# Twelve lines at the two ends of an encoder trunk kernel: how x, the gains and the first weights are loaded, and who makes four of the first eight high parts and two of the last four sums

## The chip, the cores and the metric

The kernel runs on one core of one Trainium2 chip. The metric is the device time of one execution in microseconds (us): 1946.46 us before, the median of three runs (1946.46, 1948.36 and 1946.42). TensorE (PE) does the matmuls; VectorE (DVE), ScalarE (ACT) and GpSimd (POOL) work elementwise; the queues of SyncE (SP) and of ACT issue DMAs, which 16 DMA engines carry.

## The reference

Four layers over 256 positions of width 1024 in float32. Each layer is a SwiGLU block, a token mixer (attention, spatial gating, differential attention, attention again) and another SwiGLU block, each between two norms and added to x:

```python
for i in range(DEPTH):
    g = norm_g[i]
    x = x + 0.5 * rms_norm(swiglu(rms_norm(x, g[0]), ff1_w_in[i], ff1_w_out[i]), g[1])
    ...
    x = x + rms_norm(m, g[3])
    x = x + 0.5 * rms_norm(swiglu(rms_norm(x, g[4]), ff2_w_in[i], ff2_w_out[i]), g[5])
return x
```

The change touches only how the first `x * g[0]` is prepared and how the very last `x + ...` is added and sent out.

## The kernel before

x lives in SBUF as `xr`, 128 partitions by KD = 8 blocks (k = 0 to 7) of S = 256 positions. Every operand of a matmul is cut into a high part and a low part (float32r); a product is three matmuls: high by high, high weight by low x, low weight by high x. For weights, `Stream.split` does it piece by piece (a piece is 128 x 1024): ACT casts the high part (`w_hi`, line 126), DVE subtracts to get the low part (`w_lo`, line 129). Only piece 0 is cut in two halves of 512 columns, so that its first four blocks (k = 0 to 3) can be used before the rest. For x, `Normed.high` (ACT, line 319) multiplies a block by its gain and rounds, and `Normed.low` (DVE, line 334) makes the remainder; both write into `xp`.

The start. SP's queue issues, in this order: x blocks 0 and 1, the first half of piece 0, its second half, x blocks 2 to 4, x blocks 5 to 7, piece 1, then two pieces of the second weight tile; later weight tiles (line 103) wait for their buffer. ACT's queue issues all gains as one DMA (line 197). DVE halves two of the six gain vectors of each layer (line 227) as soon as the gains are there, before anything else that needs data. PE runs 19 matmuls on a constant tile, the fillers (line 237), then the first product (`project_pair`, line 526), block by block in the order of k for piece 0, with two, one or no fillers between its first matmuls (`DUMMY`); pieces 1 to 3 follow with no filler. `Normed.begin` sets the order on ACT and DVE: the high and low part of block 0, then `W.split()` for piece 0 (both halves), then blocks 1 to 7, then pieces 1 to 3 between the squares for the norm.

The end. After the last projection `finish` spreads the norm factor with a matmul (line 258). Then `Update.multiply` (line 473, DVE, reading the factor from PSUM) makes the update of two blocks, `Update.add` (line 479) adds it to `xr`, and SP sends those two blocks out (line 1188); a loop of four turns does this, with the multiply of the next two blocks issued ahead of the add of the present two. The updates lie in tiles with the tag `upd`, of which there are two buffers. The order on PE, DVE and ACT is the order in which the code is written; on SP and POOL a scheduler sets it.

In what follows m(a) is the multiply and a(a) the add of blocks a and a + 1, with a = 0, 2, 4, 6.

Of the kernel before, what the change touches and what calls it, by code (L numbers as in the profile page):

```python
# [13 lines left out]
ALU = mybir.AluOpType  # L14
# [5 lines left out]
DEPTH = 4  # L20
KD = D // P
# [9 lines left out]
PIECE = 1024  # L31
# [25 lines left out]
def encoder_trunk_kernel(  # L57
# [14 lines left out]
    nc = tc.nc  # L72
# [121 lines left out]

    xr = act.tile([P, KD, S], F32, tag="xr", name="xr")
    g_sb = const.tile([P, DEPTH, 6, KD], F32, name="g_sb")
    nc.scalar.dma_start(g_sb, gains)
    W.load()

    def load_x(a, b):  # L200
        nc.sync.dma_start(xr[:, a:b, :], x_t[:, a:b, :])

    def load_w(c, a, b):
        nc.sync.dma_start(W.raws[c][:, a:b], w[c][:, a:b])

    load_x(0, 2)
    load_w(0, 0, PIECE // 2)
    load_w(0, PIECE // 2, PIECE)
    load_x(2, 5)
    load_x(5, KD)  # L210
    load_w(0, PIECE, WC)
    W.load()
    load_w(1, 0, PIECE)
# [52 lines left out]
    class Normed:  # L266
# [36 lines left out]
        def begin(self, gain):  # L303

            for k in range(KD):
                self.high(gain, k, k + 1)
                self.low(gain, k, k + 1)
                if k == 0:
                    W.split()
            for i in range(3):  # L310
                W.split()
                W.settle()
                for a in ((0, 2, 4), (6,), ())[i]:
                    self.square(a)
            self.total()
# [149 lines left out]
    class Update:  # L465
# [9 lines left out]
            )  # L475
            self.t[a] = t

        def add(self, a, b):
            nc.vector.tensor_tensor(xr[:, a:b, :], xr[:, a:b, :], self.t.pop(a), op=ALU.add)  # L479

    LARGE = {"h0": 4 * D, "h1": 2 * D, "l0": 2 * D, "l1": 4 * D}

# [695 lines left out]
    update = None  # L1178
    for l in range(DEPTH):
        update = ffn(l, 0, update, Ahead(g_sb[:, l, 2, :], True))  # L1180
        update = mixers[l % 3](l, l // 3, update)
        update = ffn(l, 1, update, Ahead(g_sb[:, l + 1, 0, :]) if l + 1 < DEPTH else None)
    update.multiply(0, 2)
    for a in range(0, KD, 2):
        if a + 2 < KD:
            update.multiply(a + 2, a + 4)
        update.add(a, a + 2)
        nc.sync.dma_start(out[:, a:a + 2, :], xr[:, a:a + 2, :])


# [73 lines left out]
```

## Time and profile before

| | us |
|---|---|
| median of three runs | 1946.46 |
| the profiled execution, its own time | 1947.0 |
| span of that execution, first to last instruction | 1945.3 |
| TensorE busy in the span | 1931.1 (99%) |
| VectorE busy | 1378.4 (71%) |
| ScalarE busy | 1169.6 (60%) |
| GpSimd busy | 5.2 (under 1%) |

The span is the time between the first and the last instruction; 1.7 us of the execution lie around it. A busy share is an average over the whole span; the change concerns the first 13 us and the last 9 us, which have to be read by themselves.

### The profile page before, as it was taken

To read this page: it belongs to the slowest core of one execution; us is meant where nothing else is said; L and a number is where in the kernel's file an instruction comes from. 1 tells how busy PE (TensorE), PEld (TensorE's weight loads), DVE (VectorE), ACT (ScalarE), POOL (GpSimd) and SP (SyncE) were. 2 spreads that over 40 slices of the span, in tenths; PEclk is the share of its full clock that TensorE was granted. 3 is DMA by queue.
4 is the path that set the end of the run, shared out by engine and by line. 5 is a ranking of instruction groups with operands and counts; after the bars stand their busy time and mean duration, and the time that the engine had idled before them with its cause. 6 is when DMAs were issued, how large, how long until landed. Compare 5 with 4: busy or idle time off the path is not lost.

```text
span 1945.3 us, 30035 instructions
## 1 busy us (share of the span) xinstructions
PE 1931.1 (99%) x12402; PEld 1745.4 (90%) x12402; DVE 1378.4 (71%) x1883; ACT 1169.6 (60%) x1805; POOL 5.2 (0%) x19
## 2 busy tenths in 40 slices
PE   9999999999999999999999999999999999999998
PEld 8888999888988889888988899988898888999887
DVE  6775867866777577877677668786767766868763
ACT  6655657656655565756565565675656555656552
POOL 0000000000000000000000000000000000000000
PEclk9999999999999999999999999999999999999999
DMA  7555524655455543655455544255545554535551
GB/s 262 205 184 202 190 108 154 232 189 184 171 196 186 205 163 141 216 195 182 165 195 195 195 155 174 109 200 196 188 155 213 180 206 161 197 123 183 203 201 44
DMA packets 50393, 350.30 MB, mean 180 GB/s; under 512 B 5712, under 2 KB 5968, under 8 KB 9040
## 3 DMA queue, kind: packets, MB, share of 16 engines
q1 hardware_dynamic: 48096, 341.86, 49.0%
q10 hardware_dynamic: 2160, 6.52, 0.9%
q8 instruction: 97, 1.59, 0.3%
q14 instruction: 40, 0.33, 0.1%
HBM read 347.31 MB, written 1.05 MB: 179 GB/s over the span
## 4 chain that ended last, share of the span: by engine, by line
PE 98%; DVE 1%; ACT 0%; DMA 0%; ACTq 0%; issue 0%; SPq 0%; DVEq 0%
PE pp_t L182 68%; PE pp_t L526 8%; PE pp_t L168 7%; PE pp_t L507 4%; PE pp_t L691 3%; PE pp_t L650 2%; PE pp_t L731 1%; PE pst_t L763 1%; PE pst_t L243 1%; PE pp_t L448 1%; PE pst_t L258 1%; PE pst_t L448 1%; PE pp_t L885 0%; PE pp_t L446 0%; DVE upd L473 0%; DMA w_raw<-in_w 0%
## 5 line engine op out<-in xcount | busy, mean ns | idle before, releaser
L129 DVE TENSOR_TENSOR w_lo<-w_raw,w_hi 128x1024 fp32r<-128x1024 f32 (+1 forms) x649 | 776.4, 1218 | 69.6 <-ACT w_hi L126 69.6
L126 ACT CAST w_hi<-w_raw 128x1024 fp32r<-128x1024 f32 (+1 forms) x649 | 668.9, 1046 | 160.1 <-PE pp_t L182 130.7
L182 PE MATMUL pp_t<-xp,w_hi 128*128 128x512 f32 x2560 | 613.7, 391 | 0.0
L182 PEld LDWEIGHTS pp_t<-xp,w_hi 128*128 128x128 f32 x2560 | 469.7, 188 | 90.4
L182 PEld LDWEIGHTS pp_t<-xp,w_lo 128*128 128x128 f32 x2560 | 329.0, 191 | 12.5
L182 PE MATMUL pp_t<-xp,w_lo 128*128 128x256 f32 x2560 | 334.6, 283 | 0.0
L597 DVE TENSOR_TENSOR gu<-pp_t,share 128x512 f32<-128x512 f32 x160 | 110.7, 692 | 206.1 <-ACT share L596 206.1
L596 ACT COPY share<-pp_t 128x512 f32<-128x512 f32 x160 | 93.6, 585 | 150.5 <-PE pp_t L182 149.5
L182 PE MATMUL pp_t<-h,w_hi 128*128 128x512 f32 x672 | 169.0, 391 | 0.0
L182 PE MATMUL pp_t<-l,w_hi 128*128 128x512 f32 x560 | 142.6, 391 | 0.0
L182 PEld LDWEIGHTS pp_t<-h,w_hi 128*128 128x128 f32 x672 | 122.1, 189 | 22.6
L567 ACT ACTIVATE gs<-gs 128x512 f32<-128x512 f32 x88 | 55.7, 633 | 141.5 <-DVE gs L566 141.5
L526 PE MATMUL pp_t<-xp,w_hi 128*128 128x256 f32 x832 | 123.8, 288 | 1.6 <-ACT xp L319 0.8
L182 PEld LDWEIGHTS pp_t<-l,w_hi 128*128 128x128 f32 x560 | 102.5, 188 | 21.1 <-DVE l L576 1.6
L526 PEld LDWEIGHTS pp_t<-xp,w_hi 128*128 128x128 f32 x832 | 111.1, 193 | 3.7 <-ACT xp L319 1.0
L364 DVE TENSOR_TENSOR yg<-pp_t,share 128x256 f32<-128x256 f32 x56 | 23.8, 425 | 108.8 <-ACT share L363 108.8
L182 PEld LDWEIGHTS pp_t<-h,w_lo 128*128 128x128 f32 x672 | 91.1, 191 | 5.0
L182 PE MATMUL pp_t<-h,w_lo 128*128 128x256 f32 x672 | 95.1, 282 | 0.0
L182 PE MATMUL pp_t<-l,w_lo 128*128 128x256 f32 x560 | 80.6, 283 | 0.0
L319 ACT ACTIVATE xp<-xr,g_sb 128x256 fp32r<-128x256 f32 x96 | 44.8, 504 | 56.4 <-DVE xr L479 54.0
L182 PEld LDWEIGHTS pp_t<-l,w_lo 128*128 128x128 f32 x560 | 75.3, 191 | 2.9
L526 PE MATMUL pp_t<-xp,w_lo 128*128 128x256 f32 x416 | 73.8, 284 | 0.0
(196 smaller groups left out, 2255.7 us busy)
## 6 DMA issues: line engine op xcount, KB each, us to landing
w_raw<-in_w SPq DMA_DIRECT2D x322, 1024.0 KB, 4.8
l<-in_a_bias ACTq DMA_DIRECT2D x8, 512.0 KB, 8.3
w_raw<-in_w SPq DMA_DIRECT2D x3, 512.0 KB, 8.5
out_y<-xr SPq DMA_DIRECT2D x4, 256.0 KB, 2.1
xr<-in_x_t SPq DMA_DIRECT2D x2, 384.0 KB, 6.7
w_raw<-in_w SPq DMA_DIRECT2D x2, 256.0 KB, 4.6
l<-in_b_ws ACTq DMA_DIRECT2D x1, 512.0 KB, 5.4
l<-in_b_ln_g ACTq DMA_DIRECT2D x1, 512.0 KB, 7.2
```

Of the source, the lines that this page charges most:

```text
L126: nc.scalar.copy(hi[:, cols], raw[:, cols])
L129: nc.vector.tensor_tensor(lo[:, cols], raw[:, cols], hi[:, cols].bitcast(F32), op=ALU.subtract)
L168: nc.tensor.matmul(o, w_[:, at + i, :], x(k)[:, low, :], start=(start and i == 0 and m == 0), stop=(stop and k == ks[-1] and m == 2),)
L182: nc.tensor.matmul(o[:, 0:S] if low else o, (wl if low else wh)[:, at + i, :], x(k)[:, 0, :] if low else x(k), start=(start and i == 0 and ...
L319: nc.scalar.activation(self.h[:, k, :], xr[:, k, :], AF.Copy, scale=gain[:, k:k + 1])
L448: nc.tensor.matmul(o[:, 0:S], w_, x, start=first, stop=last, skip_group_check=True)
L507: nc.tensor.matmul(o, part[:, k, :], n.x[:, k, int(low), :], start=((k, low) == JOIN[0] and i == 2 and part is ws[i][0]), stop=((k, low) = ...
L526: nc.tensor.matmul(o, part[:, k, :], n.x[:, k, low, :], start=(at == 0), stop=(at == 3 * KD - 1))
L567: nc.scalar.activation(gs, gs, AF.Silu)
L596: nc.scalar.copy(share, ps[:, :, S:2 * S])
L597: nc.vector.tensor_tensor(at.t[:, e], ps[:, :, 0:S], share, op=ALU.add)
L691: nc.tensor.matmul(self.ps[:, t, :], xs[:, kk, t * P:(t + 1) * P], ws, start=((kk, low) == self.order[0] and ws is wh and not (t == 0 and ...
```

## The change

Loads: x comes as two halves (blocks 0 to 3, blocks 4 to 7) with the whole of piece 0 as one DMA between them. The gains come as three DMAs on ACT's queue: the vector that the first norm needs, the other five of layer 0, and layers 1 to 3. High parts: the odd blocks 1, 3, 5 and 7 of the first norm are multiplied on GpSimd. Piece 0 is cast after block 2 and not after block 0. End: the adds of blocks 0 and 1 and of blocks 4 and 5 go to GpSimd.

```diff
-    nc.scalar.dma_start(g_sb, gains)
+    nc.scalar.dma_start(g_sb[:, 0, 0, :], gains[:, 0, 0, :])
+    nc.scalar.dma_start(g_sb[:, 0, 1:6, :], gains[:, 0, 1:6, :])
+    nc.scalar.dma_start(g_sb[:, 1:DEPTH], gains[:, 1:DEPTH])
...
-    load_x(0, 2)
-    load_w(0, 0, PIECE // 2)
-    load_w(0, PIECE // 2, PIECE)
-    load_x(2, 5)
-    load_x(5, KD)
+    load_x(0, 4)
+    load_w(0, 0, PIECE)
+    load_x(4, KD)
...
             for k in range(KD):
-                self.high(gain, k, k + 1)
+                if k % 2 == 0:
+                    self.high(gain, k, k + 1)
+                else:
+                    nc.gpsimd.tensor_scalar_mul(self.h[:, k, :], xr[:, k, :], gain[:, k:k + 1])
                 self.low(gain, k, k + 1)
-                if k == 0:
+                if k == 2:
                     W.split()
...
-        def add(self, a, b):
-            nc.vector.tensor_tensor(xr[:, a:b, :], xr[:, a:b, :], self.t.pop(a), op=ALU.add)
+        def add(self, a, b, engine=nc.vector):
+            engine.tensor_tensor(xr[:, a:b, :], xr[:, a:b, :], self.t.pop(a), op=ALU.add)
...
-        update.add(a, a + 2)
+        update.add(a, a + 2, nc.gpsimd if a % 4 == 0 else nc.vector)
```

Line 334 becomes line 337, line 473 becomes 476, line 479 becomes 482 and line 1188 becomes 1191. Between the first product and the last loop every engine's instructions stand in the same order as before.

On DVE at the start, before: from the halving of the gains to the low part of block 2 (`xp` rows are the low parts, block by block; `w_lo` rows are the two halves of piece 0; the names DMAHW0 to 7 are semaphores of DMAs).

```order
L227 TENSOR_SCALAR g_sb<-g_sb 128x4x8 [waits DMAHW0_49]
L227 TENSOR_SCALAR g_sb<-g_sb 128x4x8
L334 SCALAR_TENSOR_TENSOR xp<-xr,g_sb,xp 128x256 [waits DMAHW1_49,Activation_49]
L129 TENSOR_TENSOR w_lo<-w_raw,w_hi 128x512 [waits DMAHW2_49,Activation_49]
L129 TENSOR_TENSOR w_lo<-w_raw,w_hi 128x512 [waits DMAHW3_49,Activation_49]
L334 SCALAR_TENSOR_TENSOR xp<-xr,g_sb,xp 128x256 [waits Activation_49]
L334 SCALAR_TENSOR_TENSOR xp<-xr,g_sb,xp 128x256 [waits DMAHW4_49,Activation_49]
```

And the same stretch of DVE now:

```order
L227 TENSOR_SCALAR g_sb<-g_sb 128x4x8 [waits DMAHW3_49,DMAHW2_49]
L227 TENSOR_SCALAR g_sb<-g_sb 128x4x8
L337 SCALAR_TENSOR_TENSOR xp<-xr,g_sb,xp 128x256 [waits DMAHW1_49,DMAHW0_49,Activation_49]
L337 SCALAR_TENSOR_TENSOR xp<-xr,g_sb,xp 128x256 [waits Pool_49]
L337 SCALAR_TENSOR_TENSOR xp<-xr,g_sb,xp 128x256 [waits Activation_49]
L129 TENSOR_TENSOR w_lo<-w_raw,w_hi 128x512 [waits DMAHW4_49,Activation_49]
L129 TENSOR_TENSOR w_lo<-w_raw,w_hi 128x512 [waits Activation_49]
L337 SCALAR_TENSOR_TENSOR xp<-xr,g_sb,xp 128x256 [waits Pool_49]
```

The halving now waits for the second and third gains DMA, the low parts of blocks 0, 1 and 2 all stand ahead of the first low weights, and those of blocks 1 and 3 wait for GpSimd; the two halves of piece 0 wait for one DMA.

On DVE at the end, before: the four multiplies (`upd<-yg`) and the four adds (`xr<-xr`), in the order m(0), m(2), a(0), m(4), a(2), m(6), a(4), a(6).

```order
L473 TENSOR_TENSOR upd<-yg,pst_t 128x512 [waits PE_49]
L473 TENSOR_TENSOR upd<-yg,pst_t 128x512 [waits DVE_49]
L479 TENSOR_TENSOR xr<-xr,upd 128x512 [waits DVE_49]
L473 TENSOR_TENSOR upd<-yg,pst_t 128x512 [waits DVE_49]
L479 TENSOR_TENSOR xr<-xr,upd 128x512
L473 TENSOR_TENSOR upd<-yg,pst_t 128x512 [waits DVE_49]
L479 TENSOR_TENSOR xr<-xr,upd 128x512
L479 TENSOR_TENSOR xr<-xr,upd 128x512 [waits DVE_49]
```

DVE at the end now, m(0), m(2), m(4), a(2), m(6), a(6):

```order
L476 TENSOR_TENSOR upd<-yg,pst_t 128x512 [waits PE_49]
L476 TENSOR_TENSOR upd<-yg,pst_t 128x512 [waits DVE_49]
L476 TENSOR_TENSOR upd<-yg,pst_t 128x512 [waits Pool_49]
L482 TENSOR_TENSOR xr<-xr,upd 128x512 [waits DVE_49]
L476 TENSOR_TENSOR upd<-yg,pst_t 128x512 [waits Pool_49]
L482 TENSOR_TENSOR xr<-xr,upd 128x512 [waits DVE_49]
```

Two adds have left DVE. Both m(4) and m(6) now wait for GpSimd: m(4) for a(0), whose update held the buffer that it takes, and m(6) for GpSimd's second add, a(4). On SP the outputs of GpSimd's two adds now stand first (blocks 0 and 1, then 4 and 5), those of DVE's two adds behind them.

## Rows read from the trace of the kernel before

**Rows 1.** The page of the profiled execution: busy time, share of the span and instructions of each engine; and the chain that ended last, by engine.

```profile
PE 1931.1 (99%) x12402; PEld 1745.4 (90%) x12402; DVE 1378.4 (71%) x1883; ACT 1169.6 (60%) x1805; POOL 5.2 (0%) x19
...
PE 98%; DVE 1%; ACT 0%; DMA 0%; ACTq 0%; issue 0%; SPq 0%; DVEq 0%
```

**Rows 2.** The chain that ended last, in order of time, in the first 13 us. Columns: start in us, length in us, what.

```profile
1.72 5.20 DMA w_raw<-in_w
...
6.95 0.63 ACT w_hi L126
...
7.59 0.69 DVE w_lo L129
...
8.74 1.05 PE pp_t L526 x3
9.79 0.24 PE pp_t L237
10.03 0.71 PE pp_t L526 x3
```

**Rows 3.** The timeline of ACT, first 13 us. Columns: start in us, length in us, engine, line, operation, out<-in, shapes, count, and in brackets the idle time before it with what ended it (so in groups 4, 5 and 8 too).

```profile
0.81 0.41 ACTq L197 DMA_DIRECT2D g_sb<-in_gains  x1
1.25 1.28 ACT L217 ACT_TABLE_LOAD   x1 [1.25 <-PEq L1253]
4.22 0.51 ACT L319 ACTIVATE xp<-xr,g_sb 128x256 fp32r<-128x256 f32 x1 [1.69 <-DMA g_sb<-in_gains]
5.31 0.62 ACT L126 CAST w_hi<-w_raw 128x512 fp32r<-128x512 f32 x1 [0.58 <-DMA w_raw<-in_w]
...
8.65 2.51 ACT L319 ACTIVATE xp<-xr,g_sb 128x256 fp32r<-128x256 f32 x6 [0.68 <-DMA xr<-in_x_t]
11.06 1.03 ACT L126 CAST w_hi<-w_raw 128x1024 fp32r<-128x1024 f32 x1
```

**Rows 4.** The timeline of DVE, first 13 us.

```profile
4.22 0.27 DVE L227 TENSOR_SCALAR g_sb<-g_sb 128x32 f32<-128x32 f32 x2 [2.99 <-DMA g_sb<-in_gains]
...
5.96 0.69 DVE L129 TENSOR_TENSOR w_lo<-w_raw,w_hi 128x512 fp32r<-128x512 f32 x1 [0.72 <-ACT w_hi L126]
...
9.19 2.48 DVE L334 SCALAR_TENSOR_TENSOR xp<-xr,g_sb,xp 128x256 fp32r<-128x256 f32 x6 [0.51 <-ACT xp L319]
```

**Rows 5.** The timeline of PE, first 13 us: fillers (line 237) and the first matmuls of piece 0 (line 526).

```profile
1.26 4.02 PE L237 MATMUL pp_t<-filler 128*128 128x256 bf16 x19 [1.26 <-DVE filler L216]
5.98 0.39 PE L526 MATMUL pp_t<-xp,w_hi 128*128 128x256 f32 x1 [0.70 <-ACT w_hi L126]
...
6.56 0.28 PE L237 MATMUL pp_t<-filler 128*128 128x256 bf16 x1
6.71 0.39 PE L526 MATMUL pp_t<-xp,w_lo 128*128 128x256 f32 x1
6.93 0.29 PE L237 MATMUL pp_t<-filler 128*128 128x256 bf16 x1
```

**Rows 6.** DMA issues on SP's queue in the first 3.3 us: which, count, KB of each, median us from issue to landing (x blocks 0 and 1; the two halves of piece 0; piece 1; x blocks 5 to 7).

```profile
xr<-in_x_t SPq DMA_DIRECT2D x1, 256.0 KB, 3.2
...
w_raw<-in_w SPq DMA_DIRECT2D x2, 256.0 KB, 4.6
...
w_raw<-in_w SPq DMA_DIRECT2D x1, 512.0 KB, 7.7
xr<-in_x_t SPq DMA_DIRECT2D x1, 384.0 KB, 6.9
```

**Rows 7.** Stretches of 1 us: length, busy time of each engine, then the granted clock of TensorE (1.00 is 2.4 GHz, 0.50 is 1.2 GHz), the DMA engines' busy share and GB/s.

```profile
1.50:2.50 1.00, 1.00 (x6) 0.70 (x5) 0.00 (x0) 1.00 (x1) 0.00 (x0) 1.00 0.42 96
2.50:3.50 1.00, 1.00 (x7) 0.73 (x5) 0.00 (x0) 0.03 (x1) 0.00 (x0) 1.00 0.98 338
3.50:4.50 1.00, 1.00 (x7) 0.69 (x6) 0.27 (x2) 0.28 (x1) 0.00 (x0) 1.00 0.91 269
4.50:5.50 1.00, 0.78 (x5) 0.37 (x3) 0.48 (x1) 0.41 (x2) 0.00 (x0) 1.00 1.03 205
5.50:6.50 1.00, 0.52 (x4) 0.47 (x4) 0.54 (x1) 0.43 (x1) 0.00 (x0) 1.00 0.71 174
6.50:7.50 1.00, 0.72 (x5) 0.40 (x4) 0.15 (x1) 0.56 (x2) 0.00 (x0) 1.00 0.94 303
7.50:8.50 1.00, 0.48 (x2) 0.28 (x2) 0.91 (x2) 0.47 (x2) 0.00 (x0) 0.92 1.01 409
8.50:9.50 1.00, 0.86 (x4) 0.76 (x3) 0.49 (x2) 0.85 (x3) 0.00 (x0) 0.50 1.05 431
...
11.50:12.50 1.00, 1.00 (x9) 1.00 (x9) 0.55 (x2) 1.00 (x2) 0.00 (x0) 0.87 1.08 447
```

**Rows 8.** The timeline of DVE in the last 10 us: multiplies (line 473) and adds (line 479).

```profile
1936.99 1.28 DVE L473 TENSOR_TENSOR upd<-yg,pst_t 128x512 f32<-128x512 f32 x2 [0.80 <-PE pst_t L258]
...
1940.24 0.69 DVE L473 TENSOR_TENSOR upd<-yg,pst_t 128x512 f32<-128x512 f32 x1
1940.85 1.29 DVE L479 TENSOR_TENSOR xr<-xr,upd 128x512 f32<-128x512 f32 x2
```

**Rows 9.** Groups of GpSimd's instructions: line, operation, shape, count, busy us, mean ns of one, idle time before.

```profile
L932 POOL TENSOR_SCALAR_AFFINE_SELECT l<-l 128x1024 f32<-128x1024 f32 x1 | 1.2, 1197 | 483.5 <-PE pp_t L691 483.5
...
masks.py:199 POOL TENSOR_SCALAR_AFFINE_SELECT ident<-ident 128x128 f32<-128x128 f32 x1 | 0.3, 292 | 0.1
```

## The prediction

> **What bounds the kernel now.** I read the page first: TensorE is busy 99% of the span, and 98% of the chain that ended last runs through it [rows 1]. The middle is not touched by the change, so its 1.93 ms stay, and what is won or lost at either end passes straight into the time. Next the chain of the first 13 us [rows 2]: TensorE works without a gap only from 8.74 us. Ahead of that stand the DMA of the second half of weight piece 0 (1.72 to 6.92), its cast on ScalarE at 6.95, its low part on VectorE at 7.59 and the low part of block 1. So the start is bound by a landing and two casts behind it. The timelines of ScalarE, VectorE and TensorE say the same from the other side: the first cast of weights starts at 5.31 [rows 3], its low part at 5.96 [rows 4], TensorE starts at 5.98, can run block 0 and not much else, and idles again [rows 5]. Last the end: from 1936.99 VectorE does four multiplies and four adds in a row and is done at 1940.85 + 1.29 = 1942.14 [rows 8]; one output DMA and the end of the program follow.
>
> **The start, part by part.** Call C the time at which ScalarE starts the first cast of piece 0; it was 5.31 for the first half and 6.95 for the second. From C on the path is the cast, the low part and a matmul: the cast of 5.31 was followed by the first matmul with low weights at 6.71 [rows 3, 5], so TensorE can run on at C + 1.40. At that point it has four more things to do than it had left at 8.74: the low-weight matmul of block 0, a filler, the first matmul of block 1, a filler. At the lower clock one of these costs about 0.24 (0.71 for three, 0.24 for a filler [rows 2]), together 0.95; at the higher one, by the steps from 6.56 to 6.71 to 6.93 [rows 5], about 0.15 to 0.22, together 0.6 or less. The granted clock falls from 1.00 to 0.50 at about 8.3 [rows 7], after a stretch in which TensorE was busy only half the time; the change leaves it idle for longer in that stretch, so I let it fall at the same point. The change at the start is then C + 1.40 + 0.95 - 8.74 = C - 6.39 for a C above 6.9, and it is zero for a C of about 6.6, where some of the four still run at the higher clock.
>
> When does piece 0 land? Ahead of it now stand 512 KB of x, and 96 KB of gains go beside it, so 1147 kB have to move (x 524, piece 0 524, gains 98). Before, 1082 kB had moved by 6.5 and 1218 by 6.95 (the stretches of [rows 7] added up: 96, 338, 269, 205, 174, then 0.45 of 303). Early end: at the best rate of those stretches, 431 GB/s, 1147 kB take 2.7 us from about 1.8 on. But C then stops mattering: the third gains DMA is issued 2 x 0.41 later than the only one was [rows 3], so it lands at about 4.22 + 0.82 = 5.04, and on VectorE the halving (0.27) and three low parts (2.48 for six, so 1.28) now stand ahead of the first low weights [rows 4]. These start at 6.59 at the earliest, as if C were 5.94: TensorE runs on from 7.34, does some eight things at the higher clock before it falls, and gains 8.74 + 4 x 0.24 - 8.34 = 1.4. Late end: the engines serve several transfers at once. The 885 kB up to the end of piece 0's second half had moved by 5.4 (703 by 4.5, and 182 of the next 205), and its cast came at 6.95, 1.55 later, because packets of the x behind it went in between. With the same lag 1147 kB, moved by 6.71, give C = 8.27 and a loss of 1.9. I take C = 6.9, the row nearest to it: at 6.95 the whole of piece 0 was there once before, and 1218 kB had moved. The start then **loses 0.5 us**, between a gain of 1.4 and a loss of 1.9.
>
> The other edits of the start I cost at nothing, with this cover. ScalarE's two further DMA issues push its table load from 1.25 to 2.1, over at 3.4, before the first x at 4.2 [rows 3]; without the cover 0.8. SP has two issues fewer. GpSimd's high part of block 1 stands ahead of VectorE's low part of block 1 and so of the low weights. No row has such an operation; the nearest are GpSimd's selects, 0.29 for 128 and 1.20 for 1024 elements per partition [rows 9], so 256 lie between 0.29 and 1.20, by interpolation near 0.42. It starts with x at 4.2 to 5.3, and must end 0.9 (two low parts) before C + 0.65 = 7.55: up to 1.3 is hidden. Blocks 5 and 7 follow the second half of x. Before, the last x landed 6.9 us after its issue, about 9.6 [rows 6]; the same bytes lie ahead of it now, and TensorE needs block 4 only eight matmuls and two fillers after 9.25, at 11.5. Next late is the second half of the first weight tile: it landed 7.7 us after its issue [rows 6], about 10.8, its cast began at 11.06 [rows 3], and ScalarE, with four high parts less to make, is free before that.
>
> **The end, part by part.** Two adds leave VectorE, but the order shows that they stay on the path: m(4) waits for GpSimd's a(0) and m(6) for its a(4). The chain becomes m(0), a(0), m(4), a(4), m(6), a(6): four operations of VectorE (0.69 each [rows 8]) and two of GpSimd (d each), with four hops between the engines. A hop is 0.03 to 0.05 (the cast 5.31 + 0.62 = 5.93, VectorE starts at 5.96 [rows 3, 4]). Sum: 4 x 0.69 + 4 x 0.05 + 0.03 + 2d = 2.99 + 2d, against 1942.14 - 1936.99 = 5.15 before, so the change is 2d - 2.16. No row has d, a GpSimd sum of two inputs of 512 elements per partition. Lower bound: one input of 512, interpolated between the selects [rows 9], 0.68: a gain of 0.8. Upper bound: 1024 elements read one after the other, 1.20: a loss of 0.24. I take 1.1, near the row with as many elements read, so **nothing (+0.04)**. On this the Trainium skill, page "GPSIMD Engine Reference", section "Performance versus the Vector engine", speaks against the change: it has the two-input sum 1.96 times slower than on VectorE, 4497 ns for 2048 elements, by which d is 1.12 (an estimate) and the sum would be +0.08; no row here shows it. The outputs come in the order 0, 4, 2, 6; the last is released by a(6) as before.
>
> **The sum.** The profiled execution took 1947.0, 0.5 above the median. Start +0.5, end 0.0: 1947.5 on its scale, **1947.0** on that of the median.
>
> **The rivals.** *A. The data come early and GpSimd is quick.* C at its floor (-1.4) and d = 0.68 (-0.8): 1946.46 - 2.2 = 1944.3; half of it, 1945.4, if only one holds. For: fewer and longer pieces, and a DMA rate that was only 174 to 205 GB/s from 4.5 to 6.5 but 409 and more from 7.5 [rows 7]. Against: nothing in the change touches the cause of that slow stretch as far as the rows show. *B, slower: the x behind it holds up piece 0.* Before, a first half of 256 KB could start the work at 5.31 whatever became of the rest; now the first cast waits for the last packet of 512 KB, with 512 KB of x on the queue right behind. Decides from C = 6.6; at the lag seen before it is C = 8.27, +1.9: 1948.4. For: the 1.55 us lag above, and the first x landing after 3.2 but the halves of piece 0 after 4.6 in the median [rows 6]. *C. GpSimd and VectorE share a way into SBUF.* a(2) on VectorE starts just before a(4) on GpSimd; if a(4) waits until a(2) is over, 0.69 - 0.05 = 0.64 is added: 1947.6. Neither engine's rows overlap with such operations before, so the trace can't say. (The Trainium skill, page "SBUF — State Buffer", has it as an exclusive lock: a VectorE operation with two SBUF inputs and a GpSimd operation that reads SBUF block each other for the whole instruction.) *D. GpSimd's high parts are slow*, p each: above 1.3 every us delays the first low weights by one, and with blocks 5 and 7 (9.6 + 2p + 0.5 against 12.6) a second time; slower by over 0.2% from a p of about 3.3, over twice the largest row [rows 9]. *E. The clock does not fall at 8.3*: it is back at about 11.75 (0.87 in the mean of 11.5 to 12.5 [rows 7]), so nearly 3 us at half speed become whole, -1.5, 1945.5. *F. The change has no effect that can be seen* is the forecast's neighbour: 1946.5.
>
> **How the numbers follow.** Forecast with F 0.45, A 0.22, B 0.15, C 0.13, E 0.03, D 0.02. The range reaches from between A's two ends to above B, 1944.7 to 1948.9; outside lie A with both parts, D, and B with C on top. A measurement of this kernel can tell about 0.2% (3.9 us) from no change: faster than 1942.6 or slower than 1950.4. All cases but D end inside, whatever their sign: faster 0.02, same 0.95, slower 0.03.
>
> **What would show it.** In the profile after: the first cast of `w_hi` (right at 6.6 to 7.3; below 6.2 A, above 8 B); TensorE gapless from about 9.2 instead of 8.74; the high parts on GpSimd near 0.4 each; the low parts of blocks 0 to 2 over before that cast's end. At the end: m(4) and m(6) each starting right behind a GpSimd add; d near 1.1; the last add over 5.1 to 5.3 us after the first multiply begins (4.4 for A, 5.8 for C). Wrong above all if piece 0 lands much earlier, or if GpSimd takes several us for its first operation.

## The result and the profile after

| | before | after |
|---|---|---|
| median of 11 runs, us | 1947.40 (1945.11 to 1948.48) | 1952.35 (1951.56 to 1952.99) |
| after / before, 95% interval | | 1.0027 [1.0018, 1.0036] |
| the profiled execution, its own time | 1947.0 | 1952.57 |
| its span | 1945.3 | 1950.8 |
| start of block 1's second matmul | 8.74 | 12.46 |
| first multiply of the end | 1936.99 | 1941.78 |
| end of the last add | 1942.14 | 1947.78 |

The changed kernel is slower by 5 us, and 1952.35 lies above the range of 1944.7 to 1948.9. The span is 5.5 longer. Of these 3.72 have come together by block 1's second matmul, 1.07 more by the first multiply (1941.78 - 1936.99 = 4.79), 0.85 from there to the end of the last add (6.00 against 5.15), and what follows is 0.14 shorter (3.02 against 3.16).

The timeline of VectorE in the first 14 us of the changed kernel, the rows that answer to [rows 4]:

```profile
9.19 0.27 DVE L227 TENSOR_SCALAR g_sb<-g_sb 128x32 f32<-128x32 f32 x2 [7.97 <-DMA g_sb<-in_gains]
9.36 1.51 DVE L337 SCALAR_TENSOR_TENSOR xp<-xr,g_sb,xp 128x256 fp32r<-128x256 f32 x3
10.79 1.28 DVE L129 TENSOR_TENSOR w_lo<-w_raw,w_hi 128x512 fp32r<-128x512 f32 x2
```

VectorE does nothing for 7.97 us, until the gains have landed that it halves; before, the halving ran at 4.22 [rows 4]. The three low parts and the low weights queue behind it. ScalarE's timeline, beside [rows 3], shows that neither x nor the weights are late:

```profile
4.68 0.91 ACT L322 ACTIVATE xp<-xr,g_sb 128x256 fp32r<-128x256 f32 x2 [1.20 <-DMA g_sb<-in_gains]
6.67 1.14 ACT L126 CAST w_hi<-w_raw 128x512 fp32r<-128x512 f32 x2 [1.08 <-DMA w_raw<-in_w]
```

The first cast is at 6.67, and what the first norm needs of the gains was there at 4.68. GpSimd's timeline, with the high parts of blocks 1 and 3 (0.92 each):

```profile
4.75 1.82 POOL L309 TENSOR_SCALAR xp<-xr,g_sb 128x256 fp32r<-128x256 f32 x2 [3.38 <-DMA g_sb<-in_gains]
```

The DMA view of the same 14 us (queue q1 is SP's, q10 ACT's: packets, MB, share of the 16 engines' time; then the issues with KB and us from issue to landing):

```profile
q1 hardware_dynamic: 990, 4.11, 78.4%
q10 hardware_dynamic: 432, 0.10, 3.2%
...
g_sb<-in_gains ACTq DMA_DIRECT2D x1, 72.0 KB, 7.4
g_sb<-in_gains ACTq DMA_DIRECT2D x1, 20.0 KB, 5.6
g_sb<-in_gains ACTq DMA_DIRECT2D x1, 4.0 KB, 3.9
```

The same view before:

```profile
q10 hardware_dynamic: 144, 0.10, 2.6%
...
g_sb<-in_gains ACTq DMA_DIRECT2D x1, 96.0 KB, 3.4
```

Before, the whole 96 KB went as 144 packets and landed 3.4 after the issue. Now the same bytes are 432 packets. With issues at 0.79, 1.24 and 1.72 the three land at 4.7, 6.8 and 9.1: one every 2.1 to 2.3 us, whether it carries 20 KB or 72.

TensorE's timeline, which answers to [rows 5], and the 1-us stretches (granted clock third from the end), which answer to [rows 7]:

```profile
1.25 3.54 PE L237 MATMUL pp_t<-filler 128*128 128x256 bf16 x19 [1.25 <-DVE filler L216]
7.34 0.58 PE L529 MATMUL pp_t<-xp,w_hi 128*128 128x256 f32 x1 [2.55 <-ACT w_hi L126]
...
9.90 0.58 PE L529 MATMUL pp_t<-xp,w_hi 128*128 128x256 f32 x1 [1.52 <-DVE xp L337]
...
11.53 0.58 PE L529 MATMUL pp_t<-xp,w_lo 128*128 128x256 f32 x1 [0.81 <-DVE w_lo L129]
...
12.46 0.56 PE L529 MATMUL pp_t<-xp,w_hi 128*128 128x256 f32 x1
```

```profile
7.00:8.00 1.00, 0.66 (x3) 0.46 (x3) 0.00 (x0) 0.80 (x2) 0.00 (x0) 0.67 1.04 376
...
16.00:17.00 1.00, 1.00 (x7) 1.00 (x6) 1.00 (x2) 1.00 (x2) 0.00 (x0) 0.50 0.60 115
17.00:18.00 1.00, 1.00 (x8) 1.00 (x8) 1.00 (x2) 1.00 (x2) 0.00 (x0) 0.71 0.93 393
```

TensorE is idle from 4.79 to 7.34, waits twice for VectorE, and only from 11.53 runs without a gap. The clock falls to 1.2 GHz in the stretch of 7 to 8, at about 7.3 by its mean of 0.67, and is back in that of 17 to 18, at about 17.6 by its mean of 0.71; before it was low from about 8.3 to 11.75 [rows 7]. Work at half speed behind block 1's second matmul therefore lasts from 12.46 to 17.6 in place of 8.74 to 11.75, 5.1 against 3.0 us. Half of the difference is 1.06, but that this meets the 1.07 above is chance. Later, in the middle of the span, TensorE waits for low weights in both kernels; the matmul that ends this wait, before and in the changed kernel:

```profile
742.60 0.58 PE L650 MATMUL pp_t<-h,w_lo 128*128 128x256 f32 x1 [3.13 <-DVE w_lo L129]
```

```profile
747.08 0.39 PE L653 MATMUL pp_t<-h,w_lo 128*128 128x256 f32 x1 [3.13 <-DVE w_lo L129]
```

They are 4.48 apart, so 0.76 of the 1.07 had come by then and 0.31 comes behind it.

The end: VectorE's timeline, then GpSimd's, beside [rows 8]:

```profile
1941.78 1.29 DVE L476 TENSOR_TENSOR upd<-yg,pst_t 128x512 f32<-128x512 f32 x2 [0.80 <-PE pst_t L258]
1943.92 0.69 DVE L476 TENSOR_TENSOR upd<-yg,pst_t 128x512 f32<-128x512 f32 x1 [0.85 <-POOL xr L482]
1944.53 0.69 DVE L482 TENSOR_TENSOR xr<-xr,upd 128x512 f32<-128x512 f32 x1
1946.36 0.69 DVE L476 TENSOR_TENSOR upd<-yg,pst_t 128x512 f32<-128x512 f32 x1 [1.15 <-POOL xr L482]
1947.09 0.69 DVE L482 TENSOR_TENSOR xr<-xr,upd 128x512 f32<-128x512 f32 x1
```

```profile
1942.62 1.26 POOL L482 TENSOR_TENSOR xr<-xr,upd 128x512 f32<-128x512 f32 x1 [278.90 <-DVE upd L476]
1944.69 1.64 POOL L482 TENSOR_TENSOR xr<-xr,upd 128x512 f32<-128x512 f32 x1 [0.80 <-DVE upd L476]
```

m(4) and m(6) start right behind GpSimd's sums, as forecast; the sums take 1.26 and 1.64.

### The profile page after: what moved, and what is told of

Its sections match the earlier page's. It is cut to its first block, busy times and chain, and to the rows that moved or that the text cites. A ratio compares the mean times of both kernels' runs of the same rounds, so it can differ in the third digit from the quotient of the medians.

```text
span 1950.8 us, 30037 instructions
## 1 busy us (share of the span) xinstructions
PE 1932.5 (99%) x12402; PEld 1746.5 (90%) x12402; DVE 1376.6 (71%) x1881; ACT 1168.1 (60%) x1801; POOL 11.6 (1%) x25
## 4 chain that ended last, share of the span: by engine, by line
PE 97%; DVE 1%; ACT 0%; DMA 0%; issue 0%; POOL 0%; POOLq 0%; ACTq 0%; SPq 0%
PE pp_t L182 67%; PE pp_t L529 8%; PE pp_t L168 7%; PE pp_t L510 4%; PE pp_t L694 3%; PE pp_t L653 2%; PE pp_t L734 1%; PE pst_t L766 1%; PE pst_t L243 1%; PE pp_t L451 1%; PE pst_t L258 1%; PE pst_t L451 1%; PE pp_t L888 0%; DMA xr<-in_x_t 0%; DVE w_lo L129 0%; PE pp_t L449 0%
```

## The experiments

Theory G: the loss at the start comes from the gains, whose three DMAs land late and hold VectorE at the halving. Its rivals: the order of x and the weights, GpSimd's high parts, and TensorE's clock by itself. All were timed beside the kernel before (its medians here are 1947.48, 1947.43 and 1946.95); the ratio is the recorded estimate with its interval, not the quotient of the two medians. "Block 1" below is the start of block 1's second matmul, 8.74 before and 12.46 after; "end" is first multiply to end of last add.

| kernel | median of 11, us | ratio to before, 95% | halving | first low weights | block 1 | first multiply | end |
|---|---|---|---|---|---|---|---|
| one_gains | 1948.0 | 1.0002 [0.9993, 1.001] | 5.33 | 7.37 | 9.25 | 1935.42 | 5.98 |
| late_halving | 1949.16 | 1.0005 [0.9996, 1.0014] | late | 7.28 | 9.35 | 1938.58 | 5.99 |
| gains_only | 1949.44 | 1.0009 [1.0001, 1.0018] | 7.78 | 8.35 | 10.09 | 1939.58 | 5.14 |
| tail_only | 1948.15 | 1.0003 [0.9994, 1.0012] | 4.09 | 5.75 | 8.41 | 1938.38 | 5.99 |
| two_gains | 1949.97 | 1.0011 [1.0003, 1.002] | 7.04 | 8.41 | 10.08 | 1939.22 | 5.99 |
| act_highs | 1948.25 | 1.0004 [0.9995, 1.0013] | late | 7.18 | 8.95 | 1938.16 | 5.99 |
| fill | 1946.83 | 0.9998 [0.9989, 1.0007] | late | 7.18 | 8.44 | 1936.04 | 6.00 |
| tail_free | 1947.27 | 0.9997 [0.9988, 1.0005] | 4.12 | 5.56 | 8.49 | 1936.31 | 4.33 |
| x_order | 1947.23 | 1.0 [0.9991, 1.0009] | 4.94 | 7.69 | 9.76 | 1938.74 | 5.13 |
| before_fill | 1946.44 | 0.9996 [0.9987, 1.0005] | 4.77 | 6.03 | 8.88 | 1936.34 | 5.13 |
| fill_dve_tail | 1946.19 | 0.9994 [0.9985, 1.0003] | late | 7.41 | 8.66 | 1936.35 | 5.14 |
| best | 1945.96 | 0.9994 [0.9985, 1.0003] | late | 7.21 | 8.47 | 1936.25 | 4.29 |

"late" means that the halving stands behind the first norm's work. The first low weights are those of piece 0's first half (5.96 before); in gains_only, tail_only, tail_free and before_fill this half has a DMA of its own, as before, and elsewhere it comes with the whole piece. Between block 1 and the first multiply lies 1.93 ms of the same work in which the clock differs from one execution to the next (last section), so a start is read from its own rows and not from the first multiply alone.

### one_gains: the changed kernel with one gains DMA

```diff
-    nc.scalar.dma_start(g_sb[:, 0, 0, :], gains[:, 0, 0, :])
-    nc.scalar.dma_start(g_sb[:, 0, 1:6, :], gains[:, 0, 1:6, :])
-    nc.scalar.dma_start(g_sb[:, 1:DEPTH], gains[:, 1:DEPTH])
+    nc.scalar.dma_start(g_sb, gains)
```

> The changed kernel with all gains again as one DMA. Theory G (VectorE's halving of the gains waits for three gains DMAs, and everything of VectorE stands behind it): the halving starts near 5 us instead of 9.2, the first low weights near 7.4 instead of 10.8, TensorE reaches the second matmul of block 1 at 8.6 to 9.2 instead of 12.5; 1948.0 to 1948.8 us with the end's loss of 0.85 still in it. Rival W (the start is late because piece 0 lands whole, behind twice the x, and GpSimd's high parts are slow): that matmul still after 11 us, time above 1950.5.

VectorE's timeline:

```profile
5.33 0.28 DVE L225 TENSOR_SCALAR g_sb<-g_sb 128x32 f32<-128x32 f32 x2 [4.12 <-DMA g_sb<-in_gains]
5.87 1.57 DVE L335 SCALAR_TENSOR_TENSOR xp<-xr,g_sb,xp 128x256 fp32r<-128x256 f32 x3 [0.27 <-ACT xp L320]
7.37 1.28 DVE L129 TENSOR_TENSOR w_lo<-w_raw,w_hi 128x512 fp32r<-128x512 f32 x2
```

One line given back takes 3.4 us from the first low weights (10.79 to 7.37) and 3.2 from block 1, and the median is 4.35 below the changed kernel's (1948.0 to 1948.8 was expected). This is the forecast's start: cast at 6.61, low weights behind it without a wait for gains.

### late_halving: three gains DMAs, but nothing of the first norm waits for two of them

```diff
-    for i in (1, 5):
-        nc.vector.tensor_scalar_mul(g_sb[:, :, i, :], g_sb[:, :, i, :], 0.5)
...
         n = Normed(update, g_sb[:, l, 4 * which, :])
+        if update is None:
+            for i in (1, 5):
+                nc.vector.tensor_scalar_mul(g_sb[:, :, i, :], g_sb[:, :, i, :], 0.5)
```

> The changed kernel, three gains DMAs kept, with the halving of the gains moved behind the squares of the first norm on VectorE. G: as good as with one DMA, since nobody then waits for the second and third: first low weights near 7.4, 1948.0 to 1948.8 us. W, or a theory by which the three DMAs cost by slowing x and the weights: first low weights after 9 us, above 1950 us.

The three DMAs are as late as in the changed kernel, and VectorE doesn't notice: low parts at 5.23, low weights at 7.28. So the harm is in the halving's place ahead of the low parts, not in the late bytes as such. The median, 1949.16, lies above the 1948.0 to 1948.8 that were expected: block 1 starts within 0.1 of one_gains, but the profiled executions are 3.2 apart at the first multiply, with the same work between and, by the lengths of TensorE's steps, a clock that comes back later here (the section on the fillers). (The expectation of fill compares with 9.70 in this kernel: that is the row of block 1's third matmul; the second is at 9.35.)

### two_gains: the second and third gains DMA joined

```diff
-    nc.scalar.dma_start(g_sb[:, 0, 1:6, :], gains[:, 0, 1:6, :])
-    nc.scalar.dma_start(g_sb[:, 1:DEPTH], gains[:, 1:DEPTH])
+    gf, gd = (t.rearrange("p l i k -> p (l i k)")[:, KD:] for t in (g_sb, gains))
+    nc.scalar.dma_start(gf, gd)
```

> The changed kernel with its second and third gains DMA joined: 32 B and 736 B a partition in place of 32, 160 and 576. Theory G by turns (each gains packet waits for one packet of 4 KB of the other queue, so the number of packets sets the landing): the second DMA lands about 5.6 after its issue, at 6.7 to 7.1; the halving ends at 7.1 to 7.4, the first low weights start at about 8.4, block 1's second matmul at about 10.2, time 1949.5 to 1950.5. By bytes (the gains queue gets so many bytes a microsecond): the last byte lands at 8.5 to 9 as in the changed kernel, and the time stays at 1952.

The DMA view of the first 14 us, then VectorE's timeline:

```profile
q10 hardware_dynamic: 288, 0.10, 2.9%
g_sb<-in_gains ACTq DMA_DIRECT2D x1, 92.0 KB, 5.8
```

```profile
7.04 0.27 DVE L227 TENSOR_SCALAR g_sb<-g_sb 128x32 f32<-128x32 f32 x2 [5.83 <-DMA g_sb<-in_gains]
...
8.41 1.29 DVE L129 TENSOR_TENSOR w_lo<-w_raw,w_hi 128x512 fp32r<-128x512 f32 x2
```

92 KB land 5.8 after their issue, where 20 KB took 5.6: the bytes don't matter, the number of DMAs with 144 packets each does. One DMA less brings the halving 2.15 earlier, the low weights and block 1 2.38, and the median 2.38 (that the last two are the same number is chance; the first multiply comes 2.56 earlier). A DMA takes 2.1 to 2.3 us in the changed kernel; over 16 engines its 144 packets are 9 each, some 0.24 us a packet. The Trainium skill, page "DMA: Bandwidth & Descriptors", section "Queues, rings and completion order", has each DMA engine go round between the queues packet by packet, so that a packet of one queue waits for a whole packet of the other. The landings agree with it in kind: by the changed kernel's view, a packet on SP's queue took about 0.18 us (an estimate: 78.4% of 14 us on 16 engines, over 990 packets), so that one turn each makes 1.6 us a DMA, and 2.1 to 2.3 were measured. Whether the price goes by the packets or by the DMA isn't separated, since every gains DMA here has 144 packets.

### gains_only: the kernel before with the three gains DMAs

```diff
-    nc.scalar.dma_start(g_sb, gains)
+    nc.scalar.dma_start(g_sb[:, 0, 0, :], gains[:, 0, 0, :])
+    nc.scalar.dma_start(g_sb[:, 0, 1:6, :], gains[:, 0, 1:6, :])
+    nc.scalar.dma_start(g_sb[:, 1:DEPTH], gains[:, 1:DEPTH])
```

> The kernel before with only the three gains DMAs. G: the halving starts at 7 to 9 us instead of 4.2, the low parts of block 0 and the first half of piece 0 wait for it, TensorE runs on from 10 to 11.5 instead of 8.74: 2 to 4 us slower than before, 1949.4 to 1951.4. W: within 0.5 us of before.

```profile
q1 hardware_dynamic: 1255, 3.98, 81.8%
q10 hardware_dynamic: 432, 0.10, 3.5%
g_sb<-in_gains ACTq DMA_DIRECT2D x1, 72.0 KB, 5.9
g_sb<-in_gains ACTq DMA_DIRECT2D x1, 20.0 KB, 5.5
g_sb<-in_gains ACTq DMA_DIRECT2D x1, 4.0 KB, 3.0
```

The halving starts at 7.78 and the first low weights at 8.35, not at 5.96. The median is 1.96 above the kernel before, and the interval of the ratio just excludes 1. In the profiled execution the three DMAs cost 1.35 at block 1; it is 1.43 behind at the matmul that ends the wait in the middle (744.03 against 742.60) and 2.59 at the first multiply, so that the rest comes in the middle, with the clock (last section). The third DMA lands 1.5 earlier than in the changed kernel (5.9 after its issue against 7.4), with as many gains packets but smaller ones on SP's queue (3.98 MB in 1255 packets against 4.11 in 990). With issues at 0.81, 1.25 and 1.73 the three land at 3.8, 6.8 and 7.6, 2.9 and 0.9 apart: the price of a DMA is not the same each time, which speaks against a fixed one, and the 2.1 to 2.3 are the changed kernel's. The parts don't add either: there the third DMA lands later, and three low parts instead of one stand between the halving and the low weights.

### act_highs: late_halving with all high parts on ScalarE

```diff
-                if k % 2 == 0:
-                    self.high(gain, k, k + 1)
-                else:
-                    nc.gpsimd.tensor_scalar_mul(self.h[:, k, :], xr[:, k, :], gain[:, k:k + 1])
+                self.high(gain, k, k + 1)
```

> late_halving with all eight high parts on ScalarE again, 0.5 each. If GpSimd's part of the change is worth nothing (its 0.92 a block is hidden, and so was ScalarE's 0.5): ScalarE makes four high parts from 4.69 to 6.6, the first cast stays at 6.6 to 6.7, the low weights at 7.2 to 7.5, the time at 1948.5 to 1949.5. If the high parts of blocks 1 and 3 were in the way of the cast: the cast goes to 7.2 and the time up by 0.6. If GpSimd's 0.92 was in the way: blocks 4 to 7 come earlier and the time falls to about 1948.

```profile
4.72 1.31 ACT L317 ACTIVATE xp<-xr,g_sb 128x256 fp32r<-128x256 f32 x3 [1.22 <-DMA g_sb<-in_gains]
6.54 1.14 ACT L126 CAST w_hi<-w_raw 128x512 fp32r<-128x512 f32 x2 [0.51 <-DMA w_raw<-in_w]
```

ScalarE makes the three high parts that stand ahead of the cast in 1.31 us and then waits 0.51 for the weights all the same. Giving some of them to GpSimd, which takes 0.92 for each in the changed kernel, buys nothing here; nor does it cost anything that can be measured (1948.25, just below the 1948.5 to 1949.5 expected).

### x_order: the new order of x and the first weights alone

```diff
-    load_x(0, 2)
-    load_w(0, 0, PIECE // 2)
-    load_w(0, PIECE // 2, PIECE)
-    load_x(2, 5)
-    load_x(5, KD)
+    load_x(0, 4)
+    load_w(0, 0, PIECE)
+    load_x(4, KD)
...
-                if k == 0:
+                if k == 2:
                     W.split()
```

> The kernel before with the new order of x and the first weights alone (x in two halves, piece 0 in one, first split behind block 2): one gains DMA, all high parts on ScalarE, all sums at the end on VectorE. If the loads cost only what TensorE's clock makes of the longer idle stretch: first cast at 6.5 to 6.7, block 1's second matmul at 9.4 to 9.7 against 8.74, at half clock, end stretch 5.15, time +0.5 to +1, 1947.9 to 1948.5. If the new order as such is quicker, as the change says: 8.0 to 8.7 and 1946.5 or below.

Block 1 comes 1.0 later (9.76), with the first cast at 7.04 in this execution (6.5 to 6.7 was expected); the median, 1947.23, lies below the 1947.9 to 1948.5 expected and can't be told from before. The forecast had given this part -1.4 to +1.9, and 0.5 as its value.

### fill, before_fill: thirty fillers

```diff
-WARM = 19
+WARM = 30
```

> late_halving with 30 fillers ahead of the first matmul instead of 19. Theory K (what is left of the loss at the start is TensorE's clock: idle from 5.47 to 7.30, it runs the next 6.3 us at half speed): the fillers reach to 6.6 to 7.8, the steps of blocks 0 to 6 take about 0.45 us each instead of 0.88, block 1's second matmul is at 8.8 to 9.2 instead of 9.70, and up to 3 us come back: 1946 to 1947. Rival (the clock falls some microseconds after the start whatever stood there): the same steps of 0.88 from 7.3 to 7.8 on, 1949 to 1949.5, and later still if the fillers reach past the first cast.

> The kernel before with 30 fillers instead of 19, nothing else. Theory K (the fillers keep the clock up whatever the loads): TensorE is busy to about 6.3, its first real matmul comes at 6.1 to 6.4 instead of 5.98, the steps from 8.74 on take 0.45 a block instead of 0.88, first multiply of the end 1.0 to 1.7 earlier than 1936.99, time 1946 to 1946.8. Rival (the gaps at 7.2 to 8.7 bring the clock down all the same): steps of 0.88 from 8.74 to 11.7 as before, time 1947.4.

TensorE's timeline in late_halving, then in fill (fillers, and two of the steps from one block to the next):

```profile
1.24 4.23 PE L235 MATMUL pp_t<-filler 128*128 128x256 bf16 x19 [1.24 <-DVE eps_t L225]
...
9.35 0.56 PE L527 MATMUL pp_t<-xp,w_hi 128*128 128x256 f32 x1
...
10.23 0.56 PE L527 MATMUL pp_t<-xp,w_hi 128*128 128x256 f32 x1
```

```profile
1.25 5.08 PE L235 MATMUL pp_t<-filler 128*128 128x256 bf16 x30 [1.25 <-DVE eps_t L225]
...
8.44 0.36 PE L527 MATMUL pp_t<-xp,w_hi 128*128 128x256 f32 x1
...
8.91 0.36 PE L527 MATMUL pp_t<-xp,w_hi 128*128 128x256 f32 x1
```

A block with its filler takes 0.88 in the one and 0.47 in the other. With the idle stretch ahead of the first real matmul cut from 1.82 to 0.87 us, the work runs at the steps of 2.4 GHz from the start, block 1 comes 0.9 earlier (8.44; 8.8 to 9.2 was expected) and the first multiply 2.5. The medians differ by 2.3, but the intervals of the two ratios overlap. In before_fill the clock stays up as well; the steps of block 2 and on are short, and the first multiply is 0.65 earlier, where 1.0 to 1.7 was expected: TensorE then waits for the low parts (0.21 at 8.88), and gives part of the gain back. Its time can't be told from the kernel before. The fillers don't decide it alone: of the ten profiled kernels with 19 of them, nine run the first blocks at half speed and one, tail_free, does not (1936.31 is owed to that); all four with 30 run them at full speed. So the fillers make the full clock likelier, by these fourteen executions; by how much in the median isn't settled.

### tail_only, tail_free, fill_dve_tail, best: the end

tail_only is the kernel before with the change's lines of the end. tail_free adds buffers to it, for m(4) and m(6):

```diff
-        def multiply(self, a, b):
-            t = tmp.tile([P, 2, S], F32, tag="upd", name="upd")[:, 0:b - a, :]
+        def multiply(self, a, b, tag="upd", bufs=None):
+            t = tmp.tile([P, 2, S], F32, tag=tag, name="upd", bufs=bufs)[:, 0:b - a, :]
...
-            update.multiply(a + 2, a + 4)
+            update.multiply(a + 2, a + 4, *(("hf", 3) if a else ()))
```

fill_dve_tail is fill with all four sums on VectorE. best is fill with tail_free's buffers and one sum on GpSimd:

```diff
-        update.add(a, a + 2, nc.gpsimd if a % 4 == 0 else nc.vector)
+        update.add(a, a + 2, nc.gpsimd if a == 2 else nc.vector)
```

> The kernel before with only the two GpSimd sums at the end. Theory S (two GpSimd sums in series on the path): last add over 6.0 us after the first multiply begins instead of 5.15, 0.85 us slower than before: 1948.2. Rival (the end is hidden or costs nothing, all of the loss is the start's): 5.2 us, no change.

> The kernel before with the GpSimd sums at the end, and the multiplies of blocks 4 and 6 in buffers of their own, so that neither waits for a GpSimd sum. Theory W (the end is longer because m(4) and m(6) wait for a buffer that the slow sums hold): VectorE does six operations of 0.69 in a row, 4.1 us; both GpSimd sums lie beside them; from the first multiply to the end of the last add 4.1 to 4.6 instead of 5.99, and the sums keep 1.26 to 1.64. Rival P (GpSimd and VectorE shut each other out while both have two inputs in SBUF): a(2) or a(6) starts only when a GpSimd sum is over, or the sums stretch to 2 us and more, and the stretch stays at 5.2 or above. Time by W about 1946.6, by P 1947.5 to 1948.2.

> fill (the change with the halving moved behind, 30 fillers) with all four sums of the end on VectorE again. The end stretch goes from 6.0 to 5.15, block 1's second matmul stays at 8.4 to 8.5 at full clock: 0.8 below fill, 1945.8 to 1946.2, 1.2 to 1.6 below the kernel before. If the loss at the end were not from the sums: 1946.8 as fill.

> fill with GpSimd making one sum alone, that of blocks 2 and 3, and the multiplies of blocks 4 and 6 in buffers of their own: VectorE has seven operations in a row, 4.6 to 4.9 from the first multiply to the last add (5.15 before, 6.0 after). In tail_free the stretch was 4.33, but the last two outputs came 0.5 apart and the second waited for the first; here they come 0.7 apart. If the outputs take the gain: last output lands 6.6 to 6.8 after the first multiply as before, time as fill_dve_tail; if not, 6.3 to 6.5 and 0.3 less, 1945.6.

tail_only has the end of the changed kernel, 5.99, with the start of before: the 0.85 is the sums' own. (Its median is 0.67 above the kernel before, within the interval.) fill_dve_tail undoes it, 5.14. In tail_free, by VectorE's timeline:

```profile
1936.31 1.88 DVE L473 TENSOR_TENSOR upd<-yg,pst_t 128x512 f32<-128x512 f32 x3 [0.80 <-PE pst_t L258]
1938.11 0.85 DVE L479 TENSOR_TENSOR xr<-xr,upd 128x512 f32<-128x512 f32 x1
...
1939.60 1.04 DVE L479 TENSOR_TENSOR xr<-xr,upd 128x512 f32<-128x512 f32 x1
```

The waits for GpSimd's buffer are gone and the end is 4.33: it was the two buffers of `upd` that put the slow sums on the path. But little of the 0.8 reaches the time: the median, 1947.27, is not the 1946.6 expected, and the span runs on for 8.2 us from the first multiply, against 8.3 before. The SP queue's issues in before_fill or fill_dve_tail begin 1.91 after the first multiply (1938.26); in tail_free 2.13 (1938.44); in best, with the end at 4.29 (4.6 to 4.9 was expected), 3.04. GpSimd's timeline and SP's in best, then stretches of 1 us:

```profile
1937.68 1.58 POOL L480 TENSOR_TENSOR xr<-xr,upd 128x512 f32<-128x512 f32 x1 [277.79 <-DVE upd L474]
```

```profile
1939.29 1.81 SPq L1192 DMA_DIRECT2D out_y<-xr  x4
```

```profile
1940.00:1941.00 1.00, 0.00 (x0) 0.00 (x0) 0.54 (x1) 0.00 (x0) 0.00 (x0) 1.00 0.87 315
1941.00:1942.00 1.00, 0.00 (x0) 0.00 (x0) 0.00 (x0) 0.00 (x0) 0.00 (x0) 1.00 1.04 389
1942.00:1943.00 1.00, 0.00 (x0) 0.00 (x0) 0.00 (x0) 0.00 (x0) 0.00 (x0) 0.95 0.93 344
```

In best no output is issued before GpSimd's sum ends at 1939.26, though VectorE's first sum was over at 1938.14, and then 1 MB goes out without a break until about 1943, 6.7 after the first multiply. Before, the last stretch with output is that of 1943 to 1944, 0.79 busy, which makes 6.8. The outputs take the gain: those of GpSimd's sums stand first on SP's queue, and the others wait behind them. fill_dve_tail and best have the lowest medians, 0.8 to 1.0 below the kernel before beside them (1.2 to 1.6 was expected of the first), and neither can be told from it.

## Why the prediction was wrong

**The step that failed** is the place of the third gains DMA: "issued 2 x 0.41 later than the only one was, so it lands at about 4.22 + 0.82 = 5.04". I moved the landing of one DMA by the time of two issues, as if three DMAs cost no more than one but for their issues. It landed 7.4 after its issue, at 9.1: beside the long packets of x and the weights each of the three took 2.1 to 2.3 us, whatever its bytes. (That a packet waits for a packet is the likely reason; shown is the price of a DMA.) With 5.04 the halving and three low parts were hidden behind the cast, and the floor was 6.59; with 9.1 they are the path: 9.19, then low weights at 10.79. one_gains and late_halving take the step out in two independent ways, and 3.4 to 3.5 us of the low weights' delay go; two_gains takes out one DMA of the three and 2.38 of the time. No rival had it: rival B looked for the delay in the queue that carries x and the weights, and it was in the short one beside it. The two signs that the prediction named as wrong above all didn't come either: piece 0 was not early, and GpSimd's first operations took 0.92 each.

**The terms that were right.** C was 6.67 (6.9 forecast, 6.6 to 7.3 given as the mark), so the landing of piece 0 was well sized, and rival B did not come. one_gains shows the start as the forecast had it: C + 1.40 + 0.95 = 6.61 + 2.35 = 8.96, measured 9.25. That the forecast with C = 6.9 was 9.25 too is luck: C came earlier, and the first matmul with low weights came at 8.35 and not at 6.61 + 1.40 = 8.01, since TensorE's own steps were at half speed from about 7.4.

**Mis-sized.** *The clock*: I let it fall at 8.3 and return at 11.75 as before; in the changed kernel it was low from about 7.3 to 17.6, and behind block 1 another 0.76 had been lost by the middle of the span. Even without the gains' delay the longer idle stretch ahead of the first matmul is paid for at half speed: block 1 comes at 9.35 in late_halving and at 8.44 in fill, and the first multiply 2.5 us apart in the profiled executions. The forecast counted four items at half speed, 0.95, and took the rest as equal to before. *d*: 1.1 was taken and 1.20 was the upper bound, from GpSimd operations with one input; the sums took 1.26 and 1.64, and 2.99 + 2.90 = 5.89 is near the measured 6.00. The form of the sum held; the loss was 0.85 and not 0.04, by 2 x 0.16 for d itself, 0.38 for rival C below, and the 0.11 left over for longer hops between the engines. *p*: 0.92 a high part, not 0.42; it was hidden, as costed, since 1.3 lay under cover.

**Rival C** came. The sum beside m(2), which has one input in SBUF and one in PSUM, took 1.26; a(4), which started 0.16 behind a(2), took 1.64, 0.38 more, where 0.64 had been priced for a start 0.05 behind. tail_free and best have four more such pairs, in which a VectorE sum (two inputs in SBUF, 0.69 undisturbed) and a GpSimd sum (1.26) meet:

| kernel | first | starts behind it | overlap, us | the later one is longer by |
|---|---|---|---|---|
| changed | a(2), VectorE | a(4), GpSimd | 0.52 | 0.38 |
| tail_free | a(0), GpSimd | a(2), VectorE | 0.31 | 0.17 |
| tail_free | a(2), VectorE | a(4), GpSimd | 0.59 | 0.45 |
| tail_free | a(4), GpSimd | a(6), VectorE | 0.49 | 0.35 |
| best | a(0), VectorE | a(2), GpSimd | 0.45 | 0.32 |

Whichever engine starts second pays, by the overlap less some 0.14 us each time. The Trainium skill, page "SBUF — State Buffer", section "SBUF: two separate sides", has the later one wait for the whole instruction of the first. These five agree with it but for the 0.14, for which no run shows a reason.

What is not settled: how much of the 5 us is the clock's in each single execution, because it differs between executions.

## What to carry to other kernels

Cutting a small load into several DMAs on a queue of its own brings its first part a little earlier and its last part much later when another queue is full of long packets: here the first gains served at 4.68 in place of 5.33 in one_gains, and the last landed at 9.1 in place of 5.3. So price such a load by its DMAs and packets, not by its bytes, and look at who waits for the last of them. Before an engine's queue is loaded at the start, move every operation that isn't needed yet (here a halving of 0.27 us) behind the path; its own price is small, its wait is not. A sum given to a slower engine is only free if its buffer isn't the next one wanted, if its output doesn't hold up the other outputs, and if no operation of the other engine that reads two inputs from SBUF meets it.

## What the runs showed that I had not expected

Three small DMAs of 4, 20 and 72 KB landed 2.1 to 2.3 us apart, and one of 92 KB no later than one of 20 KB (5.8 against 5.6 after the issue).

In late_halving and x_order the column of the granted clock stands at 1.00 throughout the first 13 us, though a block takes 0.88 there and 0.47 in fill. The traces of these two hold no clock record before 13.6 and 13.9 us, and the column counts a time without a record as 1.00; the steps tell the level.

TensorE waits 3.1 us in the middle, in the spatial gating, in every kernel, and the clock falls behind it in some executions and not in others: the stretch of 745 to 750, in gains_only and then in one_gains,

```profile
745.00:750.00 5.00, 5.00 (x26) 5.00 (x25) 2.65 (x5) 0.89 (x2) 0.00 (x0) 0.51 0.60 213
```

```profile
745.00:750.00 5.00, 5.00 (x44) 5.00 (x44) 2.16 (x4) 3.40 (x4) 0.00 (x0) 1.00 0.33 136
```

In the first, 26 matmuls run in the 5 us, in the second 44. This, and where the clock returns at the start, goes with a spread of up to 4 us between executions of one kernel (late_halving: 1945.43 to 1949.4), and it is why differences under 2 us could not be settled by the medians.
